# A two-layer decoder trunk on one core: low parts of the first 24 dense expert tiles of each layer made on GpSimd instead of VectorE

## The chip, the core and the metric

The kernel runs on one core of a Trainium2 chip. Time is device microseconds (us) of one execution, and less is better. TensorE (PE) multiplies, VectorE (DVE), ScalarE (ACT) and GpSimd (POOL) do the element-wise work, and SyncE (SP) starts most of the transfers from HBM. Three executions of the kernel before took 3294.35, 3295.38 and 3302.20 us; the median is 3295.38 us.

## What is computed

Two post-norm layers over 512 tokens of 1024 numbers. The first layer mixes tokens by retention, the second by differential attention, and each is followed by the same expert layer, PEER, in which the change lies:

```python
def peer_ffn(x, w_q, subkeys, u, v):      # per 128 tokens
    q = (xc @ w_q).reshape(128, 8, 2, 128)
    sc = einsum('thpd,hpnd->thpn', q, subkeys)
    s1, i1 = top_k(sc[:, :, 0], 16)
    s2, i2 = top_k(sc[:, :, 1], 16)
    cand = s1[..., :, None] + s2[..., None, :]
    cidx = i1[..., :, None] * 128 + i2[..., None, :]
    top, pos = top_k(cand.reshape(128, 8, 256), 16)
    idx = take_along_axis(cidx, pos)      # 8 x 16 experts of 16384
    gate = softmax(top)
    act = gelu(einsum('ted,td->te', u[idx], xc))
    return einsum('te,ted->td', gate * act, v[idx])
```

Every token picks 16 experts for each of 8 heads out of 16384. An expert is a row of `u` and a row of `v`, 1024 float32 numbers each.

## The kernel before

**Split numbers.** Matrix products are made at float32 accuracy from rounded halves. `split` (lines 102 to 104) has ACT round a tile to `h` (line 103), and then DVE, or another engine given as `eng`, subtracts to get the low part `l` (line 104). `mm3` (lines 106 to 109) adds three products, high by high, high by low and low by high. `wload` (line 111) loads a weight tile of 128x1024 into one of RING = 9 buffers `wraw` and splits it into `wh` and `wl`, of which there are three each. Weights of the query projections already get their low part on POOL, since `query_feed` hands `nc.gpsimd` to `wload`.

**The expert layer.** `peer` (line 879) treats the tokens as four blocks of 128. Block 0 is sparse: each of its 128 expert slots is one gather of rows of `u` by POOL (`ug`, line 752) and one dot product on DVE (line 754), later the same with `v` (lines 765, 767). Blocks 1 to 3, 384 tokens, are dense: PE multiplies all 128 tiles of 128 experts with the tokens (`u_tile`, line 854, 24 products of 128x384 per tile), ACT applies gelu, and the activations are weighted with a gate matrix that DVE, ACT and PE build from one-hot rows (`gmat`, line 827).

**The stage around the change.** The first part of `peer` (pool `p1`) does three things beside each other. DVE finds the best keys of each half (`topk_keys`, lines 685 to 690), sorts the pairs of them block by block (`topk_pairs`, lines 693 to 739) and then makes the one-hot rows of `gmat`. PE works through `u` tiles 0, 1, 2 and so on; 82 of the 128 are made here in each layer. From tile 22 on, dot products of block 0 are mixed in. The loop from line 941 gives the sequence: for each planned piece of DVE work `u_tile` calls are made until a planned tile time catches up, and the call `next(su)` issues a gather and a dot product behind the newest low part (`behind("low")`).

**Who sets the order on an engine.** The code is handed to a scheduler that orders each engine's instructions by its own model of their times. That order is fixed in the built program: an engine works its list in sequence, and an instruction that waits holds up all behind it. The program has the kernel's line numbers; `tk_` tiles belong to the pair sort, `sc` and `tk_m` to the key sort, `mu` and `rt` are the two PSUM tags that `u` tiles alternate on.

Of the kernel before, what the change touches and what calls it, by code (L numbers as in the profile page):

```python
# [54 lines left out]
OHB = 4  # L55
EQB = 2
UT = 4.0
RING = 9
SB = 4
LEAD = 4  # L60
# [3 lines left out]
def build(tc, I, out):  # L64
    nc = tc.nc
    ctx = ExitStack()
    with ctx:
# [21 lines left out]
        def bank(tag):  # L89
            return psum.tile([P, 512], F32, name=tag, tag=tag, bufs=4 if tag == "pj" else 2)  # L90
# [4 lines left out]
        def behind(*what):  # L95

            ctx = ExitStack()
            for w in what:
                ctx.enter_context(tc.issue_after(newest[w].ins))
            return ctx  # L100

        def split(h, l, src, eng=None):
            nc.scalar.activation(h, src, AF.Copy)  # L103
            newest["low"] = (eng or nc.vector).tensor_tensor(out=l, in0=src, in1=h.bitcast(F32), op=OP.subtract)  # L104

        def mm3(o, ah, al, bh, bl, start, stop):
            nc.tensor.matmul(o, ah, bh, start=start, stop=False)  # L107
            nc.tensor.matmul(o, ah, bl, start=False, stop=False)  # L108
            return nc.tensor.matmul(o, al, bh, start=False, stop=stop)  # L109

        def wload(src, eng=None, pool=None, tag="", bufs=3, dst=None):
            a = src.shape[1]
            pool = pool or wp
            raw = wp.tile([P, 1024], F32, name="wraw", tag="wraw", bufs=RING)
            nc.sync.dma_start(raw.rearrange("p (a b) -> p a b", a=a), src)
            if dst is None:
                h = pool.tile([P, 1024], F32R, name="wh", tag="wh" + tag, bufs=bufs)
                l = pool.tile([P, 1024], F32R, name="wl", tag="wl" + tag, bufs=bufs)
            else:
                h, l = dst  # L120
            split(h, l, raw, eng)
            return h.rearrange("p (a b) -> p a b", a=a), l.rearrange("p (a b) -> p a b", a=a)
# [67 lines left out]
        def lnp(l, i):  # L190
            g = wp.tile([P, D], F32, name="lng", tag="wraw", bufs=RING)
            nc.sync.dma_start(g, I["ln_g"][l, i:i + 1, :].to_broadcast([P, D]))
            b = wp.tile([P, D], F32, name="lnb", tag="wraw", bufs=RING)
            nc.sync.dma_start(b, I["ln_b"][l, i:i + 1, :].to_broadcast([P, D]))
            return g, b
# [46 lines left out]
        def retention():  # L242
            with tc.tile_pool(name="ret", bufs=1) as rp:
# [11 lines left out]
                def load_x(q):  # L255
                    xr = wp.tile([P, 1024], F32, name="wraw", tag="wraw", bufs=RING)
                    xr = xr.rearrange("p (a b) -> p a b", a=2)
                    nc.sync.dma_start(xr, I["xt"][:, 2 * q:2 * q + 2, :])
                    split(XTH[:, 2 * q:2 * q + 2, :], XTL[:, 2 * q:2 * q + 2, :], xr)
# [481 lines left out]
        def softmax(gate):  # L741
            nc.scalar.activation(gate, gate, AF.Exp)
            zs = small.tile([P, 8], F32, name="tk_z", tag="tk_z")
            nc.vector.reduce_sum(out=zs, in_=gate, axis=AX.X)
            nc.vector.reciprocal(out=zs, in_=zs)
            nc.vector.tensor_tensor(out=gate, in0=gate, in1=zs.unsqueeze(2).to_broadcast([P, 8, 16]), op=OP.mult)

        def sparse_u(kp, t, l, idx, act):
            scr = kp.tile([P, D], BF16, name="scr", tag="scr")
            for j in range(P):  # L750
                u = wp.tile([P, D], F32, name="ug", tag="wraw", bufs=RING)
                nc.gpsimd.indirect_dma_start(out=u, out_offset=None, in_=I[f"u{l}"],  # L752
# [5 lines left out]
        def sparse_v(kp, t, l, idx, gate, act):  # L758
# [4 lines left out]
            for j in range(P):  # L763
                v = wp.tile([P, D], F32, name="vg", tag="wraw", bufs=RING)
                nc.gpsimd.indirect_dma_start(out=v, out_offset=None, in_=I[f"v{l}"],  # L765
# [85 lines left out]
                nc.sync.dma_start(gd.rearrange("g p q f -> q p g f")[t0 // GT + q], st.rearrange("p (g a) t -> p g (a t)", a=GA))  # L851
                yield 6.0

        def u_tile(dp, l, a, tag="mu"):
            uh, ul = wload(I[f"ut{l}"][a])
            b = bank(tag)
            for k in range(KD):
                newest["mm"] = mm3(b[:, :DT], uh[:, k, :], ul[:, k, :], XTH[:, k, S - DT:], XTL[:, k, S - DT:], k == 0, k == KD - 1)
            act = dp.tile([P, DT], F32, name="uact", tag="uact", bufs=LEAD + 1)
            newest["gelu"] = nc.scalar.activation(act, b[:, :DT], AF.Gelu_apprx_tanh)  # L860
            return act
# [17 lines left out]
        def peer(l, norm, feed, prepare):  # L879
            with tc.tile_pool(name="sp", bufs=1) as sp, tc.tile_pool(name="dp", bufs=1) as dp:  # L880
# [6 lines left out]
                with tc.tile_pool(name="p1", bufs=1) as kp:  # L887
                    M = [kp.tile([P, 16, 16], F32, name=f"tk_m{t}") for t in range(TB)]
                    MI = [kp.tile([P, 16, 16], U32, name=f"tk_i{t}") for t in range(TB)]
                    with tc.tile_pool(name="pq", bufs=1) as qp:  # L890
                        scores(qp, M, MI, l, norm, feed)
                        if l == 0:
                            iota_f = qp.tile([P, P], F32, name="iota_f")
                            nc.sync.dma_start(iota_f, I["iota"])
                            nc.vector.tensor_copy(out=iota50,
                                                  in_=iota_f[:, :NCAND].unsqueeze(2).to_broadcast([P, NCAND, 16]))
                            nc.vector.tensor_copy(out=iota4, in_=iota_f.unsqueeze(2).to_broadcast([P, P, 4]))
                    with tc.tile_pool(name="tk", bufs=1) as tp:
                        def pairs(t, got):
                            idx = tp.tile([P, P], I32, name="tk_idx", tag="tk_idx", bufs=2)  # L900
                            gate = tp.tile([P, 8, 16], F32, name="tk_g", tag="tk_g", bufs=2)
                            yield from topk_pairs(tp, M[t], MI[t], idx, gate)
                            got.append((idx, gate))

                        def gates():


                            got = []

                            def exps():  # L910
                                with behind("gelu"):
                                    softmax(got[-1][1])

                            def rows():
                                with behind("mm"):
                                    return gate_rows(tp, got[-1][0], got[-1][1].rearrange("p h k -> p (h k)"))

                            yield from pairs(1, got)
                            yield 36.0
                            exps()  # L920
                            yield 8.0
                            nxt = rows()
                            yield 4.0
                            for t in range(1, TB):
                                now = nxt
                                more = pairs(t + 1, got) if t + 1 < TB else ()
                                for n, cost in enumerate(gmat(tp, *now, (t - 1) * P, gd, G0)):
                                    yield cost
                                    for c in (more if n == P // GT - 4 else itertools.islice(more, 2)):
                                        yield c  # L930
                                    if t + 1 < TB and n == P // GT - 3:
                                        exps()
                                    if t + 1 < TB and n == P // GT - 2:
                                        nxt = rows()

                        for _ in topk_pairs(tp, M[0], MI[0], idx0, gate0):
                            pass
                        su = sparse_u(sp, 0, l, idx0, act0)
                        nu, nd, tv, tu = 0, 0, 0.0, -40.0

                        for cost in gates():
                            tv += cost
                            while tu < tv and nu < P:
                                act = u_tile(dp, l, nu, ("mu", "rt")[nu % 2])
                                nc.sync.dma_start(ad[nu], act)
                                nu += 1
                                tu += UT
                                while nd < DOTS * (nu - LAG):
                                    with behind("low"):
                                        next(su, None)  # L950
                                    nd += 1
                                    tv += 1.2
                with tc.tile_pool(name="p2", bufs=1) as kp:
# [25 lines left out]
                    for a in range(P):  # L979
# [6 lines left out]
                        if a < nu:  # L986
                            act = kp.tile([P, DT], F32, name="aact", tag="aact", bufs=4)
                            nc.sync.dma_start(act, ad[a])
                        else:
                            act = ahead.pop(0)  # L990
# [97 lines left out]
```

## Time and profile before

| | |
|---|---|
| median of three executions | 3295.38 us |
| the profiled execution's own time | 3296.86 us |
| its span, first to last instruction | 3295.1 us |
| PE busy | 3200.2 us (97%) |
| DVE busy | 2519.7 us (76%) |
| ACT busy | 1397.7 us (42%) |
| POOL busy | 940.8 us (29%) |

The profile is one execution. The busy share of an engine is an average over stages that have different limits, so a stage is read by its own window. A row of a timeline gives the start, the duration, the engine, the line, the operation and, in square brackets, the idle time before it and what ended that.

### The profile page before, as it was taken

The numbers are of one execution on the slowest core, as the hardware profiler recorded it, in microseconds if no ns is written. First come the engines' busy times: TensorE is split into PE (matmuls) and PEld (weight loads), VectorE is DVE, ScalarE is ACT, GpSimd is POOL, SyncE is SP. The second block draws the span as 40 slices with busy tenths as digits, with TensorE's granted clock in tenths as the row PEclk, the third lists the DMA queues.
The fourth block names the chain that finished last, engine by engine and source line by source line (L and its number), as shares of the span: only waits on it lengthen the run. The fifth ranks groups of instructions, "written<-read, shape, count | busy, mean of one in ns | idle before, by whom it ended". The sixth has DMA issues, their size and how long they took to land.

```text
span 3295.1 us, 47178 instructions
## 1 busy us (share of the span) xinstructions
PE 3200.2 (97%) x16666; PEld 2844.1 (86%) x16666; DVE 2519.7 (76%) x4849; ACT 1397.7 (42%) x2436; POOL 940.8 (29%) x663
## 2 busy tenths in 40 slices
PE   9999999899989999999999999999999999999998
PEld 7888889899988888889888668989999788888987
DVE  4444468999768888888963665899986888888886
ACT  3323333367773333333333643335776333333332
POOL 1101330211112333455424423021111233345540
PEclk9999999999999999999999999999999999999999
DMA  5222233578789999999943202357878999999993
GB/s 212 86 86 85 90 94 127 183 235 259 250 267 342 360 354 349 330 359 357 352 140 92 77 26 84 120 175 235 250 257 264 336 355 365 342 334 344 354 341 134
DMA packets 310077, 774.38 MB, mean 235 GB/s; under 512 B 25936, under 2 KB 154320, under 8 KB 306256
## 3 DMA queue, kind: packets, MB, share of 16 engines
q1 hardware_dynamic: 236112, 502.89, 44.3%
q0 software_dynamic: 73728, 268.47, 22.6%
q8 instruction: 131, 2.15, 0.3%
q14 instruction: 106, 0.87, 0.1%
HBM read 692.88 MB, written 78.38 MB: 234 GB/s over the span
## 4 chain that ended last, share of the span: by engine, by line
PE 76%; DVE 12%; issue 8%; ACT 2%; DMA 1%; POOL 1%; POOLq 0%; DVEq 0%; SPq 0%; ACTq 0%
PE pj L107 13%; PE pj L108 13%; PE pj L109 13%; PE mu L109 6%; PE mu L107 6%; PE mu L108 5%; PE rt L108 5%; PE rt L107 5%; PE rt L109 5%; DVE wl L104 3%; PE pj L844 2%; DVE tk_idf L736 1%; DMA ug<-in_u,idx 1%; DVE tk_ex L733 1%; PE mu L499 1%
## 5 line engine op out<-in xcount | busy, mean ns | idle before, releaser
L103 ACT ACTIVATE wh<-wraw 128x1024 fp32r<-128x1024 f32 x632 | 659.3, 1055 | 609.9 <-PE mu L108 123.1
L104 DVE TENSOR_TENSOR wl<-wraw,wh 128x1024 fp32r<-128x1024 f32 x572 | 695.0, 1224 | 214.0 <-ACT wh L103 212.3
L752 POOL DMA_INDIRECT ug<-in_u,idx x256 | 355.5, 1389 | 1241.2 <-DVE wl L104 641.5
L107 PE MATMUL mu<-xth,wh 128*128 128x384 f32 (+1 forms) x1424 | 483.3, 340 | 25.7 <-ACT uact L860 18.4
L109 PE MATMUL mu<-xth,wl 128*128 128x384 f32 (+1 forms) x1424 | 482.3, 339 | 15.4 <-DVE wl L104 15.4
L108 PE MATMUL mu<-xtl,wh 128*128 128x384 f32 (+1 forms) x1424 | 480.3, 337 | 0.0
L765 POOL DMA_INDIRECT vg<-in_v,idx x256 | 336.1, 1313 | 329.6 <-DVE x L767 232.9
L108 PE MATMUL pj<-wl,wwh 128*128 128x512 f32 x1024 | 398.7, 390 | 0.0
L109 PE MATMUL pj<-wh,wwl 128*128 128x512 f32 x1024 | 397.2, 389 | 0.0
L103 ACT ACTIVATE wwh<-w 128x384 fp32r<-128x384 f32 x256 | 134.2, 525 | 602.2 <-issue 366.0
L107 PE MATMUL pj<-wh,wwh 128*128 128x512 f32 x1024 | 380.2, 390 | 0.0
L754 DVE CUSTOM_DVE_ANT_0 scr<-ug,x 128x1024 bf16<-128x1024 f32 x256 | 312.5, 1221 | 26.2 <-DMA ug<-in_u,idx 25.8
L767 DVE SCALAR_TENSOR_TENSOR x<-vg,wgt,x 128x1024 f32<-128x1024 f32 x256 | 328.3, 1282 | 4.2 <-DMA vg<-in_v,idx 0.7
L107 PEld LDWEIGHTS mu<-xth,wh 128*128 128x128 f32 x1424 | 271.2, 191 | 32.2 <-ACT uact L860 19.0
L109 PEld LDWEIGHTS mu<-xth,wl 128*128 128x128 f32 x1424 | 271.2, 190 | 20.4 <-DVE wl L104 20.2
L108 PEld LDWEIGHTS mu<-xtl,wh 128*128 128x128 f32 x1424 | 271.3, 191 | 3.6
L104 DVE TENSOR_TENSOR wwl<-w,wwh 128x384 fp32r<-128x384 f32 x256 | 142.7, 559 | 127.5 <-ACT wwh L103 123.0
L109 PE MATMUL rt<-xth,wl 128*128 128x384 f32 (+1 forms) x688 | 230.7, 335 | 7.2 <-DVE wl L104 7.2
L107 PE MATMUL rt<-xth,wh 128*128 128x384 f32 (+1 forms) x688 | 231.9, 338 | 0.2
L108 PE MATMUL rt<-xtl,wh 128*128 128x384 f32 (+1 forms) x688 | 230.2, 335 | 0.4 <-DVE xtl L104 0.4
L109 PEld LDWEIGHTS pj<-wh,wwl 128*128 128x128 f32 x1024 | 192.2, 188 | 40.1
L108 PEld LDWEIGHTS pj<-wl,wwh 128*128 128x128 f32 x1024 | 192.2, 188 | 38.5
(242 smaller groups left out, 6281.5 us busy)
## 6 DMA issues: line engine op xcount, KB each, us to landing
wraw<-in_ut SPq DMA_DIRECT2D x256, 512.0 KB, 4.5
wraw<-in_v SPq DMA_DIRECT2D x256, 512.0 KB, 6.9
gd<-g_st SPq DMA_DIRECT2D x48, 896.0 KB, 5.6
gl<-gd SPq DMA_DIRECT2D x28, 1536.0 KB, 9.7
ad<-uact SPq DMA_DIRECT2D x164, 192.0 KB, 3.2
aact<-ad SPq DMA_DIRECT2D x164, 192.0 KB, 5.4
wraw<-in_w_in SPq DMA_DIRECT2D x48, 512.0 KB, 4.2
wraw<-in_peer_w_q SPq DMA_DIRECT2D x32, 512.0 KB, 4.0
```

The lines of the kernel that those rows point to most:

```text
L103: nc.scalar.activation(h, src, AF.Copy)
L104: newest["low"] = (eng or nc.vector).tensor_tensor(out=l, in0=src, in1=h.bitcast(F32), op=OP.subtract)
L107: nc.tensor.matmul(o, ah, bh, start=start, stop=False)
L108: nc.tensor.matmul(o, ah, bl, start=False, stop=False)
L109: return nc.tensor.matmul(o, al, bh, start=False, stop=stop)
L499: nc.tensor.matmul(b[:, :n], qt[g][ms, h, qb * P:qb * P + P], kt[g][ms, h, :n], start=True, stop=True)
L733: nc.vector.tensor_tensor(out=ex, in0=eq, in1=cidx[:, hs, :].unsqueeze(3).to_broadcast([P, HG, NCAND, 16]), op=OP.mult)
L752: nc.gpsimd.indirect_dma_start(out=u, out_offset=None, in_=I[f"u{l}"], in_offset=bass.IndirectOffsetOnAxis(ap=idx[:, j:j + 1], axis=0))
L754: nc.vector.tensor_tensor_reduce(out=scr, in0=u, in1=X[t], scale=1.0, scalar=0.0, op0=OP.mult, op1=OP.add, accum_out=act[:, j:j + 1])
L765: nc.gpsimd.indirect_dma_start(out=v, out_offset=None, in_=I[f"v{l}"], in_offset=bass.IndirectOffsetOnAxis(ap=idx[:, j:j + 1], axis=0))
L767: nc.vector.scalar_tensor_tensor(out=X[t], in0=v, scalar=w[:, j:j + 1], in1=X[t], op0=OP.mult, op1=OP.add)
L844: nc.tensor.matmul(b[:, i * P:i * P + P], oh[:, 1, i, :], oh[:, 0, i, :], start=True, stop=True)
```

## The change

`u_tile` gets a parameter `eng`, which it hands to `wload`. In the loop of `peer` the first `EARLY` = 24 tiles of each layer pass `nc.gpsimd`, so that their low part is a subtraction on POOL; tiles 24 to 127 stay with DVE. Lines after 57 move down by two.

```diff
@@ -55,6 +55,8 @@
 UT = 4.0
+
+EARLY = 24
 RING = 9
@@ -851,8 +853,8 @@
-        def u_tile(dp, l, a, tag="mu"):
-            uh, ul = wload(I[f"ut{l}"][a])
+        def u_tile(dp, l, a, tag="mu", eng=None):
+            uh, ul = wload(I[f"ut{l}"][a], eng)
             b = bank(tag)
@@ -941,7 +943,7 @@
                             while tu < tv and nu < P:
-                                act = u_tile(dp, l, nu, ("mu", "rt")[nu % 2])
+                                act = u_tile(dp, l, nu, ("mu", "rt")[nu % 2], nc.gpsimd if nu < EARLY else None)
                                 nc.sync.dma_start(ad[nu], act)
```

The order on POOL, from the last weights of the retention to the end of the expert layer of layer 0; `ug` and `vg` are gathers, `rs_r` belongs to a layer norm. Before:

```order
L104 TENSOR_TENSOR wo<-wraw,wo 128x1024
L187 TENSOR_TENSOR rs_r<-rs_t,mhalf 128x1 x4
L104 TENSOR_TENSOR wl<-wraw,wh 128x1024 x13
L752 DMA ug<-in_u,idx_3192 128x1024 x128
L765 DMA vg<-in_v,idx_3192 128x1024 x128
```

And in the changed program:

```order
L106 TENSOR_TENSOR wo<-wraw,wo 128x1024
L189 TENSOR_TENSOR rs_r<-rs_t,mhalf 128x1 x4
L106 TENSOR_TENSOR wl<-wraw,wh 128x1024 x36
L754 DMA ug<-in_u,idx_3192 128x1024
L106 TENSOR_TENSOR wl<-wraw,wh 128x1024
L754 DMA ug<-in_u,idx_3192 128x1024 x127
L767 DMA vg<-in_v,idx_3192 128x1024 x128
```

The 13 low parts of query weights are followed by those of tiles 0 to 22, one gather, the low part of tile 23, and then the other gathers.

The order on DVE in the pair sort of block 0, from the products of positions and indices (`tk_ex`) on. Before, low parts stand between the sort's instructions:

```order
L733 TENSOR_TENSOR tk_ex<-tk_eq,tk_ci 128x1600 x2
L716 MAX tk_b<-tk_c 128x8 x8
L104 TENSOR_TENSOR wl<-wraw,wh 128x1024
L736 TENSOR_REDUCE tk_idf<-tk_ex 128x32
L104 TENSOR_TENSOR wl<-wraw,wh 128x1024
L736 TENSOR_REDUCE tk_idf<-tk_ex 128x32
L718 MAX_INDEX tk_p<-tk_b,tk_c 128x8 x8
L733 TENSOR_TENSOR tk_ex<-tk_eq,tk_ci 128x1600
```

In the changed program:

```order
L735 TENSOR_TENSOR tk_ex<-tk_eq,tk_ci 128x1600 x2
L718 MAX tk_b<-tk_c 128x8 x8
L738 TENSOR_REDUCE tk_idf<-tk_ex 128x32 x2
L720 MAX_INDEX tk_p<-tk_b,tk_c 128x8 x8
L735 TENSOR_TENSOR tk_ex<-tk_eq,tk_ci 128x1600 x2
L723 MATCH_REPLACE tk_c<-tk_b,tk_c 128x50 x8
```

The sort runs through without a low part from its beginning on.

The order on DVE around the first dot product of block 0 (`scr`, shown as ISA). Before, it stands in the middle of the second block's pair sort:

```order
L736 TENSOR_REDUCE tk_idf<-tk_ex 128x32
L104 TENSOR_TENSOR wl<-wraw,wh 128x1024
L754 ISA scr,act_3191<-ug,x_77 128x1024
L754 ISA act_3191 128x1
L736 TENSOR_REDUCE tk_idf<-tk_ex 128x32
L721 MATCH_REPLACE tk_c<-tk_b,tk_c 128x50 x8
L104 TENSOR_TENSOR wl<-wraw,wh 128x1024
```

In the changed program:

```order
L718 MAX tk_b<-tk_c 128x8 x8
L720 MAX_INDEX tk_p<-tk_b,tk_c 128x8 x8
L756 ISA scr,act_3191<-ug,x_77 128x1024
L756 ISA act_3191 128x1
L106 TENSOR_TENSOR wl<-wraw,wh 128x1024 x2
L756 ISA scr,act_3191<-ug,x_77 128x1024
L756 ISA act_3191 128x1
L106 TENSOR_TENSOR wl<-wraw,wh 128x1024
```

The two low parts behind the first dot product are those of tiles 24 and 25, the first that DVE still makes; ahead of them stand the whole pair sorts of blocks 0 and 1 and the first half (candidates and both passes for the best 16) of those of blocks 2 and 3.

## Rows read from the trace of the kernel before

**Rows 1.** The page: busy time by engine, and ACT's costliest group.

```profile
PE 3200.2 (97%) x16666; PEld 2844.1 (86%) x16666; DVE 2519.7 (76%) x4849; ACT 1397.7 (42%) x2436; POOL 940.8 (29%) x663
...
L103 ACT ACTIVATE wh<-wraw 128x1024 fp32r<-128x1024 f32 x632 | 659.3, 1055 | 609.9 <-PE mu L108 123.1
```

**Rows 2.** Waits of PE, whole run: total us, times, longest.

```profile
PE mu L109 <- DVE wl L104: 15.4, 13, 2.7
```

**Rows 3.** Busy time by window: window, its length, engines, granted clock, DMA share, GB/s.

```profile
544.00:621.00 77.00, 73.61 (x421) 72.47 (x420) 76.97 (x268) 25.60 (x36) 11.67 (x4) 1.00 0.50 163
659.00:741.00 82.00, 82.00 (x532) 82.00 (x531) 82.00 (x152) 54.52 (x112) 14.88 (x9) 1.00 0.73 235
```

**Rows 4.** Timeline of PE: first products of tiles 8, 9, 24 and 29.

```profile
557.14 0.33 PE L107 MATMUL mu<-xth,wh 128*128 128x384 f32 x1
...
561.30 0.33 PE L107 MATMUL rt<-xth,wh 128*128 128x384 f32 x1
...
632.08 0.33 PE L108 MATMUL rt<-xtl,wh 128*128 128x384 f32 x1
...
659.02 0.33 PE L108 MATMUL rt<-xtl,wh 128*128 128x384 f32 x1
```

**Rows 5.** Low parts that POOL already makes: duration ns, minimum, median, maximum.

```profile
L104 POOL TENSOR_TENSOR wl<-wraw,wh x60: 2354/2396/3007, 370.5 to 2076.3; 128x1024 fp32r<-128x1024 f32 x60
```

**Rows 6.** Groups of DVE instructions between 549.6 and 659.7 us.

```profile
L104 DVE TENSOR_TENSOR wl<-wraw,wh 128x1024 fp32r<-128x1024 f32 x23 | 28.3, 1234 | 0.8 <-ACT wh L103 0.8
L736 DVE TENSOR_REDUCE tk_idf<-tk_ex 128x32 f32<-128x1600 f32 x8 | 23.8, 2976 | 0.0
L733 DVE TENSOR_TENSOR tk_ex<-tk_eq,tk_ci 128x1600 f32<-128x1600 bf16 x8 | 14.5, 1833 | 0.0
...
L754 DVE CUSTOM_DVE_ANT_0 scr<-ug,x 128x1024 bf16<-128x1024 f32 x6 | 7.4, 1239 | 0.0
L730 DVE TENSOR_TENSOR tk_eq<-iota,tk_pb 128x1600 bf16<-128x1600 bf16 x8 | 7.4, 1003 | 0.0
```

**Rows 7.** Timeline of DVE: end of the key sort, start of the pair sort.

```profile
525.17 0.87 DVE L685 MAX8 tk_m<-sc 128x8 f32<-128x128 f32 x4 [2.68 <-ACT sc L808]
...
549.68 0.29 DVE L695 CAST tk_f<-tk_i 128x256 f32<-128x256 uint32 x1
```

**Rows 8.** Timelines of POOL and DVE where a low part on POOL meets DVE.

```profile
1802.24 2.43 POOL L104 TENSOR_TENSOR wl<-wraw,wh 128x1024 fp32r<-128x1024 f32 x1 [4.87 <-ACT wh L103]
...
1802.20 0.22 DVE L431 TENSOR_TENSOR tok<-rtmp 128x64 f32<-128x64 f32 x1
1802.33 2.42 DVE L432 TENSOR_TENSOR tok<-rtmp 128x64 f32<-128x64 f32 x1
...
451.73 2.39 POOL L104 TENSOR_TENSOR wl<-wraw,wh 128x1024 fp32r<-128x1024 f32 x1 [4.83 <-ACT wh L103]
...
452.08 0.28 DVE L687 FIND_INDEX8 tk_i<-tk_m,sc 128x8 uint32<-128x128 f32 x1
```

**Rows 9.** Timelines of POOL and DVE around three POOL instructions.

```profile
1651.36 1.55 POOL L187 TENSOR_TENSOR rs_r<-rs_t,mhalf 128x1 f32<-128x1 f32 x1 [17.23 <-DVE rs_t L185]
...
1651.25 3.50 DVE L104 TENSOR_TENSOR wl<-wraw,wh 128x1024 fp32r<-128x1024 f32 x3
...
601.85 7.20 POOL L752 DMA_INDIRECT ug<-in_u,idx  x1 [0.30 <-issue]
...
634.91 0.94 POOL L752 DMA_INDIRECT ug<-in_u,idx  x1 [4.37 <-DVE wl L104]
...
634.54 2.97 DVE L736 TENSOR_REDUCE tk_idf<-tk_ex 128x32 f32<-128x1600 f32 x1
```

**Rows 10.** A long wait of PE in its timeline, and two windows after it.

```profile
986.27 0.69 PE L107 MATMUL mu<-xth,wh 128*128 128x384 f32 x1 [9.46 <-ACT uact L860]
...
980.00:986.00 6.00, 0.00 (x0) 0.00 (x0) 5.34 (x6) 5.97 (x7) 3.24 (x2) 0.50 0.84 265
986.00:990.00 4.00, 3.73 (x12) 3.73 (x13) 4.00 (x7) 1.59 (x4) 2.63 (x3) 0.50 1.00 346
```

## The prediction, made before the changed kernel ran

> **What bounds the kernel now.** I read the page first: PE is busy for 97% of the span [rows 1], so a change on DVE or POOL counts only where PE waits for them. The list of PE's waits says where that is: for the tiles of one PSUM tag alone it waits 15.4 us, in 13 pieces, for low parts made by DVE [rows 2]. Then I read windows. During the pair sort DVE is busy for 76.97 of 77 us, while PE is not [rows 3]. From 659 us on PE is busy all the time as well, for 82.00 of 82 us [rows 3], and stays so nearly to the end of the layer. So a microsecond that PE gains or loses among the first 30 tiles of a layer is a microsecond of the end, once per layer, and the two layers look alike.
>
> How much is there? An undisturbed tile takes 561.30 - 557.14 = 4.16 us of PE [rows 4]. From tile 9 at 561.30 tile 24 could begin at 623.7 and tile 29 at 644.5. They begin at 632.08 and 659.02 [rows 4]. The stage loses 14.5 us per layer, waits and the slower clock after them together. Twice that, 29 us, is the most the change can win here.
>
> **The change, step by step.** It takes 24 subtractions per layer from DVE and gives them to POOL. Nothing is added: the same transfers, roundings and products. The scheduler, though, closes the gaps on DVE: in its new order the pair sort stands in one piece, and the low parts of tiles 24 and 25 come behind it.
>
> *POOL's own pace.* A low part takes 2.40 us on POOL [rows 5], 1.23 on DVE [rows 6]. With three buffers, tile n's can begin about 1.1 us into tile n-2, when ACT has rounded it, which takes 1.06 us [rows 1]. It then has 7.2 us until tile n begins and needs 2.4. The gathers queued behind tile 22's and 23's are not wanted before DVE is through its sort. I cost this at nothing; PE's patience is 4.8 us per tile, and what uses it up is a rival below.
>
> *DVE's start.* Eight low parts stand ahead of the pair sort, which begins at 549.68 [rows 7]. Three of them come before DVE runs dry and waits 2.68 us for scores [rows 7]; these win nothing. The other five, 1.14 us each from start to start, bring the sort forward by 5.7 us, to 544.0.
>
> *DVE's list up to the first dot product.* Before, the same work lay between 549.7 and 659.7 us: 110 us, with 23 low parts and 6 dot products in it [rows 6]. Without these 29 x 1.14 = 33 us it is 77 us. Undisturbed, DVE reaches the first dot product at 544 + 77 = 621 us, and tile 24's low part is ready at 623.3, just in time for 623.7.
>
> *What DVE loses to POOL.* This is where I expect the gain to go. Where a low part on POOL and an addition of two SBUF tensors on DVE meet, the DVE instruction, 0.22 us by itself, takes 2.42 us and ends with POOL's [rows 8]. A search in the key sort, which reads one tensor, takes its 0.28 us beside another low part [rows 8], and a reduction runs beside a POOL gather that still takes only 0.94 us [rows 9]. So I count as exposed what reads two SBUF tensors, with the casts: the products (8 at 1.74 us from start to start), the comparisons (8 at 0.90) and about 10 us of small additions and casts, 31 of the 77 us. The other 46 us, reductions, maxima and searches, run on.
>
> POOL makes the low parts of tiles 7 to 23 in this time: 17, one per 4.16 us, from 545.8 to 614.7. The first bound of what they cost DVE is nothing, if each falls beside a reduction or search; the second is 17 x 2.39 = 40.6 us, if each stops DVE from its first to its last moment. Between the two I take it in proportion. Of 4.16 us POOL holds 2.39, which leaves 1.77 for exposed work, so an exposed microsecond takes 2.35. In the 69 us DVE gets through y of free and 0.67 y of exposed work, with y + 0.67 y x 2.35 = 69: y = 26.7, together 44.7 us. It loses 24 us.
>
> *The sum.* DVE reaches the dot product at 544 + 77 + 24 = 645 us. With that and one low part, 1.14 us each, tile 24 begins at 647.6 instead of 632.1. PE has stood since 623.7. Five tiles later it is at 668.4 instead of 659.0: 9.4 us lost. After a long wait the clock is low for a while: after 9.46 us PE ran 3.8 us at a granted clock of 0.50, its 1.2 GHz level, up to 990.06 us, which cost 1.9 us [rows 10]. I add that, with the same row as the nearest: 11.3 us per layer, 22.6 in all. DVE's later work fits behind PE, since the list after the sort is no longer than before and PE comes later to it. On the profiled execution's 3296.9 us that makes 3319.5; the median of the runs is 1.5 us lower, so 3318. The bounds are 3266 (nothing lost) and 3350 (40.6 us lost).
>
> The break-even is worth knowing: tile 29 is on time if tile 24 begins at about 636, hence if DVE loses 13 us. **Below 13 us the change wins, above it loses.**
>
> **Rivals.**
>
> *The low parts hardly meet exposed work (faster).* If DVE loses under 5 us, PE never waits for POOL and at most 4 us at tile 24. With nothing lost tile 29 comes at 644.5, 14.5 us earlier, 29 us over two layers: 3266 against the median. With 5 us lost it is about 3276, with the clock 3280. For it: 46 of 77 us read one tensor, and reductions come in pairs of 5.8 us in the new order, long enough for a low part. Against it: the exposed work comes in blocks of up to 8 us, and POOL asks every 4.16 us.
>
> *DVE keeps POOL out through a whole run of exposed instructions (no change).* A gather that takes 0.94 us when free took 7.20, to the end of a run of additions and comparisons on DVE [rows 9]. If low parts on POOL wait like that, DVE loses only what sticks out behind a reduction or search, some 0.7 us of each, 12 in all. But then PE waits for POOL: a run of eight comparisons, products and additions lasts about 8.6 us, PE's patience is 4.8, so twice some 3 us are lost; DVE reaches the dot product at 633, and tile 29 comes near 656. Three waits, each with a spell of low clock that costs 1.7 us as those of the stage now do, make it 661, 2 us late: 3299 for two layers, between 3290 and 3305.
>
> Against that rival stands a small POOL instruction that met three low parts on DVE in a row: it ended 0.44 us after the first, while the others ran on, unlengthened [rows 9]. I take this as the more direct case, since it is an arithmetic instruction. The Trainium skill, page "SBUF — State Buffer", section "SBUF: two separate sides", says that DVE and GpSimd share a port pair that is an exclusive lock, held for one whole instruction by whoever starts first. By that rule a POOL instruction gets its turn after each DVE instruction, which is my forecast, 3318, and not 3299; the 2.42 us agree with the lock, and the 7.20 us do not agree with the turn.
>
> *Nearly every low part stops DVE in full.* 3335 to 3350; for this the proportion would have to be far off.
>
> **How the numbers follow.** About 0.3%, 10 us, is what a measurement of this kernel can tell from no change: 3285.5 to 3305.3. The forecast, 3308 to 3335 for 17 to 32 us lost, gets 0.55; DVE keeping POOL out, 3290 to 3305, gets 0.27; the gain, 3266 to 3287, gets 0.15; the full stop 0.03. Slower by over 0.3% is the forecast and the full stop, 0.58; no change is the second rival without its rim, 0.26; faster is 0.16. The range leaves out the gain and the full stop, nearly 0.2: 3286 to 3335. The forecast's own range is 3308 to 3335.
>
> **What the profile of the changed kernel would show.** PE's waits on DVE's low parts are no longer spread over the stage in pieces of 2 us: one wait of some 20 us per layer stands ahead of tile 24, with a granted clock of 0.50 behind it. DVE's products and comparisons have means well above 1.83 and 1.00 us, with single ones near 4, while reductions and searches keep theirs. The first dot product starts near 645 us. POOL's low parts stay under 4 us each. If instead their median in the sort is 5 us or more and PE waits for POOL at two places, the second rival is right. If the first dot product starts before 628 and PE runs through, the first is. I am wrong altogether if the time moves without tile 29 of layer 0 having moved, or if the second layer does something else than the first.

## The result: 0.5% slower, and the profile after

The changed kernel took 3314.77 us (median of six executions, 3307.88 to 3319.82), the kernel before, run beside it, 3298.95 us (six executions, 3294.35 to 3302.20). The ratio is 1.0051, 95% interval 1.0038 to 1.0064: slower, by 15.8 us. The prediction was 3318 us, with 0.58 on slower. The profiled execution of after is its longest, 3319.82 us.

Busy time by engine, from the page of after, answers to [rows 1]:

```profile
PE 3199.7 (96%) x16666; PEld 2848.6 (86%) x16666; DVE 2510.4 (76%) x4801; ACT 1395.9 (42%) x2436; POOL 1067.1 (32%) x711
```

PE's work is the same. DVE gave up 48 low parts of 1.23 us, 59 us, and yet its busy time fell by only 9 us: 50 us were put on it elsewhere. The waits of PE for low parts of the tag `mu`, whole run (total us, times, longest), against the 15.4 us in 13 pieces of [rows 2]:

```profile
PE mu L111 <- DVE wl L106: 50.8, 9, 23.7
```

Before, PE's waits for low parts between 500 and 800 us, the stage of layer 0, were these, 8.5 us with both tags:

```profile
PE mu L109 <- DVE wl L104: 4.9, 3, 2.7
PE rt L109 <- DVE wl L104: 3.6, 2, 2.1
```

Now the stage of each layer has a single wait, two of the nine; this is layer 0's in PE's timeline (start, duration, and in brackets the idle time and what ended it), with the first products of tile 24 ahead of it and tile 29 behind, and then layer 1's:

```profile
626.01 0.33 PE L109 MATMUL mu<-xth,wh 128*128 128x384 f32 x1
626.19 0.34 PE L110 MATMUL mu<-xtl,wh 128*128 128x384 f32 x1
650.18 0.69 PE L111 MATMUL mu<-xth,wl 128*128 128x384 f32 x1 [23.66 <-DVE wl L106]
...
675.12 0.33 PE L109 MATMUL rt<-xth,wh 128*128 128x384 f32 x1
...
2234.36 0.69 PE L111 MATMUL mu<-xth,wl 128*128 128x384 f32 x1 [21.33 <-DVE wl L106]
```

PE starts tile 24 at 626.01, does the two products that need only the high part, and stands until DVE has made the low part. The windows say the same (columns as in [rows 3]): no PE loss in the sort, where before 3.4 of 77 us were lost [rows 3], a clock of 0.50 right behind the wait, and a PE that is busy all the time from tile 29 to 757 us.

```profile
546.00:621.00 75.00, 75.00 (x435) 75.00 (x434) 74.91 (x218) 25.88 (x36) 57.14 (x19) 1.00 0.40 137
...
650.00:655.00 5.00, 4.82 (x15) 4.82 (x16) 4.99 (x9) 0.00 (x0) 2.61 (x2) 0.50 0.76 249
675.00:757.00 82.00, 82.00 (x537) 82.00 (x536) 81.11 (x109) 56.11 (x123) 14.78 (x9) 1.00 0.77 255
```

A tile is counted here by PE's products, 24 for each. That is how [rows 4] has to be read as well: the rows at 632.08 and 659.02 are the products with 24 and 29 tiles' worth of work ahead of them, and not the first products of tiles 24 and 29, since before the products of neighbouring tiles are mixed (the row at 632.08 has the tag `rt` and line 108, which belong to an odd tile and to a second product). As marks of PE's progress the rows of before and after can be compared.

One thing must be taken off before the two traces are compared. In this execution the clock was down for a moment at 392 us, ahead of the stage (window, engines, granted clock as above):

```profile
392.00:395.60 3.60, 3.60 (x10) 2.78 (x9) 1.31 (x3) 1.02 (x2) 2.36 (x1) 0.54 0.52 157
```

The first product of tile 0 starts 2.9 us late, 1.7 of it by the clock (3.60 us at 0.54). Up to 497 us all kernels here have the same instructions in the same order on PE, DVE, ACT and POOL, so this is not the change's work; nine of the eleven traces of after and of the experiments have this dip, and the one trace of before does not. PE's timeline of before, at the first product of tile 0 in layers 0 and 1, and at the first one after the stage of layer 1:

```profile
519.64 0.33 PE L107 MATMUL mu<-xth,wh 128*128 128x384 f32 x1
2093.24 0.33 PE L107 MATMUL mu<-xth,wh 128*128 128x384 f32 x1
2559.39 0.69 PE L107 MATMUL mu<-xth,wh 128*128 128x384 f32 x1 [8.94 <-ACT uact L860]
```

The row of layer 0's end stands in [rows 10], 986.27. PE's timeline of after, at the start and the end of the stage in both layers:

```profile
522.57 0.33 PE L109 MATMUL mu<-xth,wh 128*128 128x384 f32 x1
998.12 0.69 PE L109 MATMUL mu<-xth,wh 128*128 128x384 f32 x1 [9.37 <-ACT uact L862]
2109.08 0.33 PE L109 MATMUL mu<-xth,wh 128*128 128x384 f32 x1
2582.72 0.69 PE L109 MATMUL mu<-xth,wh 128*128 128x384 f32 x1 [9.97 <-ACT uact L862]
```

Layer 0 begins 2.9 us late and ends 11.9 late: the stage lost 8.9 us. Layer 1 begins 15.8 late and ends 23.3 late: 7.5 us. Together 16.4 us, against 15.8 between the medians. The rest of the 23 us between the two spans lies outside the stage, 2.9 us ahead of it and 4.0 between the two. Between the layers the clock fell at two places where before it did not (columns as in [rows 3]); the two windows of after, and below them one of before that takes in all of that stretch:

```profile
1447.00:1450.40 3.40, 2.96 (x9) 2.97 (x10) 3.37 (x4) 0.30 (x1) 2.13 (x2) 0.50 0.60 189
1518.70:1522.10 3.40, 3.40 (x12) 3.39 (x12) 3.33 (x4) 0.00 (x0) 1.81 (x2) 0.51 0.65 187
...
991.00:1867.00 876.00, 867.72 (x4119) 739.95 (x4117) 668.91 (x980) 318.66 (x493) 337.69 (x244) 1.00 0.79 289
```

The 4.0 us are not this execution's alone: in all eleven traces the stretch between the layers is 3.1 to 7.9 us longer than in the one trace of before, with spells at 0.50 between 1425 and 1590 us. Why the clock falls there, and whether other executions of before have it too, is not shown. So the stage explains the change's loss, but that 16.4 lies so near to 15.8 is in part chance: this execution is 5 us above the median of its kernel.

Where most of DVE's 50 us went (20 and 18 us in the sorts of the two layers, over the run with one eighth below) shows in its groups between the start of the sort and the first dot product (us busy, mean ns), layer 0:

```profile
L738 DVE TENSOR_REDUCE tk_idf<-tk_ex 128x32 f32<-128x1600 f32 x8 | 23.2, 2937 | 0.0
L735 DVE TENSOR_TENSOR tk_ex<-tk_eq,tk_ci 128x1600 f32<-128x1600 bf16 x8 | 14.4, 1841 | 0.0
...
L707 DVE TENSOR_TENSOR tk_c<-tk_m 128x16 f32<-128x16 f32 x12 | 10.5, 922 | 0.0
L732 DVE TENSOR_TENSOR tk_eq<-iota,tk_pb 128x1600 bf16<-128x1600 bf16 x8 | 7.4, 984 | 0.0
L697 DVE CAST tk_f<-tk_i 128x256 f32<-128x256 uint32 x4 | 5.3, 1322 | 0.1
```

Reductions, products and comparisons have the means of [rows 6]. It is the small additions of line 707 and the casts of line 697 that grew: a mean of 922 ns for 16 numbers per partition, and 1322 ns for a cast that took 0.29 us before [rows 7]. One such place in the timelines of POOL and of DVE:

```profile
560.66 11.07 POOL L106 TENSOR_TENSOR wl<-wraw,wh 128x1024 fp32r<-128x1024 f32 x3 [1.75 <-ACT wh L105]
```

```profile
560.50 0.64 DVE L707 TENSOR_TENSOR tk_c<-tk_m 128x128 f32<-128x128 f32 x4
561.05 3.70 DVE L732 TENSOR_TENSOR tk_eq<-iota,tk_pb 128x1600 bf16<-128x1600 bf16 x4
564.66 7.20 DVE L707 TENSOR_TENSOR tk_c<-tk_m 128x24 f32<-128x24 f32 x4
571.78 0.21 DVE L711 TENSOR_TENSOR tk_c<-tk_m 128x64 f32<-128x64 f32 x1
```

POOL's low part starts at 560.66 and is kept out by the rest of four additions and by four comparisons, which run at their usual pace; it takes 6.36 us, the longest in the run (POOL's low parts, minimum, median, maximum in ns):

```profile
L106 POOL TENSOR_TENSOR wl<-wraw,wh x108: 2350/2400/6362, 371.9 to 2205.2; 128x1024 fp32r<-128x1024 f32 x108
```

Then POOL gets its turn, makes three low parts end on end until 571.73, and four additions of 0.2 us take 7.20 us together: POOL's next low part was ready each time, and each of the first three additions lasted until one of them ended.

### The profile page after: what moved, and what is told of

It reads as the page before. It is cut to its first block, busy times and chain, and to the rows that moved or that the text cites. A ratio compares the mean times of both kernels' runs of the same rounds, so it can differ in the third digit from the quotient of the medians.

```text
span 3318.1 us, 47188 instructions
## 1 busy us (share of the span) xinstructions
PE 3199.7 (96%) x16666; PEld 2848.6 (86%) x16666; DVE 2510.4 (76%) x4801; ACT 1395.9 (42%) x2436; POOL 1067.1 (32%) x711
## 4 chain that ended last, share of the span: by engine, by line
PE 81%; DVE 9%; issue 6%; ACT 1%; DMA 1%; POOL 1%; POOLq 0%; SPq 0%; DVEq 0%; ACTq 0%
PE pj L109 13%; PE pj L110 13%; PE pj L111 13%; PE mu L111 6%; PE mu L109 6%; PE mu L110 6%; PE rt L110 6%; PE rt L109 6%; PE rt L111 6%; PE pj L846 3%; DVE tk_idf L738 1%; DMA ug<-in_u,idx 1%; DVE tk_c L707 1%; PE mu L501 1%; PE rt L808 1%
## 5 line engine op out<-in xcount | busy, mean ns | idle before, releaser
L106 DVE TENSOR_TENSOR wl<-wraw,wh 128x1024 fp32r<-128x1024 f32 x524 | 636.7, 1224 | 225.7 <-ACT wh L105 219.1
L754 POOL DMA_INDIRECT ug<-in_u,idx x256 | 341.5, 1334 | 1052.1 <-DVE wl L106 611.7
L106 POOL TENSOR_TENSOR wl<-wraw,wh 128x1024 fp32r<-128x1024 f32 x108 | 283.3, 2628 | 332.5 <-ACT wh L105 307.9
```

## The experiments

All kernels are edits of the changed one; the one with one eighth and the copy leave work out. In the seven rows under the change DVE's order up to the first dot product is that of the change. "Sort" is the time from the first cast of the pair sort to the first dot product, layer 0 of the one profiled execution.

| run | sort, us | median, us | ratio to before, 95% interval |
|---|---|---|---|
| the change (24 tiles) | 100.8 | 3314.8 | 1.0051 (1.0038 to 1.0064) |
| one eighth on GpSimd | 80.5 | 3275.8 | 0.9927 (0.9912 to 0.9942) |
| copy on GpSimd | 83.0 | 3282.4 | 0.9951 (0.9935 to 0.9966) |
| four pieces, 24 tiles | 91.8 | 3297.7 | 0.9997 (0.9987 to 1.0006) |
| 28 tiles | 102.5 | 3295.4 | 0.9994 (0.9984 to 1.0003) |
| two pieces, 28 tiles | 96.2 | 3285.0 | 0.9967 (0.9954 to 0.9979) |
| four pieces, 28 tiles | 96.7 | 3288.3 | 0.9974 (0.9964 to 0.9984) |
| eight pieces, 28 tiles | 109.7 | 3312.3 | 1.0049 (1.0033 to 1.0066) |
| 8 tiles (15 low parts of DVE in the sort) | 80.5 | 3291.8 | 0.9976 (0.9966 to 0.9986) |
| 14 tiles (9 low parts in it) | 90.1 | 3304.3 | 1.0017 (1.0008 to 1.0026) |
| 16 tiles (7 low parts in it) | 90.5 | 3309.7 | 1.0033 (1.0023 to 1.0043) |

The theory: GpSimd's low parts stop DVE's additions, and what DVE loses in the sort PE waits for. Its first rival: the new order costs the time by itself.

**One eighth of the work on GpSimd.**

```diff
-            split(h, l, raw, eng)
+            nc.scalar.activation(h, raw, AF.Copy)
+            p = slice(0, piece)
+            newest["low"] = (eng or nc.vector).tensor_tensor(out=l[:, p], in0=raw[:, p], in1=h[:, p].bitcast(F32), op=OP.subtract)
...
-            uh, ul = wload(I[f"ut{l}"][a], eng)
+            uh, ul = wload(I[f"ut{l}"][a], eng, piece=128 if eng else 1024)
...
-                newest["mm"] = mm3(b[:, :DT], uh[:, k, :], ul[:, k, :], XTH[:, k, S - DT:], XTL[:, k, S - DT:], k == 0, k == KD - 1)
+                newest["mm"] = mm3(b[:, :DT], uh[:, k, :], (uh if eng and k else ul)[:, k, :], XTH[:, k, S - DT:], XTL[:, k, S - DT:], k == 0, k == KD - 1)
```

> The part on GpSimd of each of the 24 low parts is cut to one eighth (128x128 in place of 128x1024); the products of the other seven eighths take the high part instead of the low one, so PE, ACT and the transfers do the same work and the low part of the weights is left out. DVE's order up to the first dot product is that of the change. Theory port (GpSimd's low parts stop DVE's additions of two SBUF tensors until they end): from the start of the pair sort to the first dot product it takes 78 to 84 us in place of 101.7, no addition takes over 0.6 us, PE waits under 5 us for tile 24's low part, and the time is 3266 to 3280 us, faster than the kernel before by 15 to 30 us. Rival order (the sort in one piece, with tile 24's low part behind it, costs the time by itself): the sort still takes over 95 us, PE still waits 20 us or more, 3305 to 3320 us. Rival handover (each instruction on GpSimd costs DVE a fixed time, however short): 95 us or more too, with additions still near 2.4 us.

The sort took 80.5 us, PE's wait shrank to 3.4 us, and the time came to 3275.8 us. DVE's groups in the sort, and PE's wait between 500 and 800 us:

```profile
L737 DVE TENSOR_TENSOR tk_ex<-tk_eq,tk_ci 128x1600 f32<-128x1600 bf16 x8 | 14.2, 1819 | 0.0
...
L709 DVE TENSOR_TENSOR tk_c<-tk_m 128x16 f32<-128x16 f32 x12 | 2.0, 218 | 0.0
...
L699 DVE CAST tk_f<-tk_i 128x256 f32<-128x256 uint32 x4 | 1.2, 300 | 0.1
```

```profile
PE mu L111 <- DVE wl L125: 3.4, 1, 3.4
```

With the same order, and the same count of GpSimd instructions, the additions are back at 218 ns and the cast at 300. So neither the order nor a fixed price per instruction costs the time; it is the time that GpSimd's instruction lasts. Without what that takes from DVE, the move of the low parts and the new order, both together, would be worth 22 us.

**Four pieces per low part.**

```diff
-            split(h, l, raw, eng)
+            nc.scalar.activation(h, raw, AF.Copy)
+            for i in range(0, 1024, piece):
+                p = slice(i, i + piece)
+                newest["low"] = (eng or nc.vector).tensor_tensor(out=l[:, p], in0=raw[:, p], in1=h[:, p].bitcast(F32), op=OP.subtract)
...
-            uh, ul = wload(I[f"ut{l}"][a], eng)
+            uh, ul = wload(I[f"ut{l}"][a], eng, piece=256 if eng else 1024)
```

> GpSimd makes each of the 24 low parts in four pieces of 128x256, the same work in shorter instructions; DVE's order is that of the change. Theory port: no addition on DVE takes over 0.8 us, since GpSimd holds the port for about 0.6 us at a time; GpSimd has to win the port four times for one low part, so DVE loses less than in the change, 8 to 20 us of sort instead of 22 to 25, and the time is 3280 to 3312 us. Rival order: no change against the changed kernel, 3310 to 3320 us. Rival handover (a fixed price per GpSimd instruction): more is lost than in the change, 3325 us or more.

91.8 us of sort, 3297.7 us, no addition over 0.85 us: as the theory had it, but for the 0.8. The four kernels with 24 tiles and one order on DVE (the copy is told below) now stand near a line: 80.5, 83.0, 91.8 and 99.6 us of sort (the last the mean of 100.8 and layer 1's 98.4) give 3275.8, 3282.4, 3297.7 and 3314.8 us. That is 39.0 us for 19.1, 2.04 us for each microsecond that DVE loses in a layer (2.6, 1.7 and 2.2 in the single steps); there are two layers. The traces say it of the stage alone: from the run with one eighth to the change it grows by 21.6 us in layer 0, for 20.3 of sort, and by 18.9 in layer 1, for 18.0. And the break-even is where a sort of 91.8 us gives the time of before.

**The copy.**

```diff
+            if copy:
+                nc.scalar.activation(h, raw, AF.Copy)
+                newest["low"] = eng.tensor_copy(out=l, in_=raw)
+            else:
+                split(h, l, raw, eng)
...
-            uh, ul = wload(I[f"ut{l}"][a], eng)
+            uh, ul = wload(I[f"ut{l}"][a], eng, copy=bool(eng))
```

> GpSimd copies the tile (one tensor read, one written) where the change subtracts; the subtraction is left out, and so the output is not that of the low parts. DVE's order up to the first dot product is that of the change. Theory whole port (whatever GpSimd does in SBUF holds DVE's additions until it ends): additions of up to the copy's own length, and a loss in the sort that is to the 22 us of the change as the copy's length is to 2.40 us, at least 5 us. Rival two operands (only GpSimd instructions that read two tensors stop DVE): no addition over 0.6 us, the first dot product 78 to 82 us after the sort's start, 3266 to 3282 us as in the run with one eighth.

Neither expectation holds in full. Three copies in the sort, from POOL's timeline:

```profile
559.25 2.55 POOL L125 CAST wl<-wraw 128x1024 fp32r<-128x1024 f32 x1 [3.11 <-PE rt L111]
563.41 3.10 POOL L125 CAST wl<-wraw 128x1024 fp32r<-128x1024 f32 x1 [1.61 <-PE mu L111]
567.58 1.05 POOL L125 CAST wl<-wraw 128x1024 fp32r<-128x1024 f32 x1 [1.06 <-PE rt L111]
```

Beside a reduction a copy takes 1.05 us; beside comparisons and products it waits, 2.55 and 3.10. Four additions of DVE lasted over 1 us, none over 1.07. So here a POOL instruction that reads one tensor meets DVE's additions too, and stops one for about its own length. But DVE lost only 2.5 us over the run with one eighth, less than the 5 that the first theory wanted, and 3282.4 us lies just above the rival's range. How much of that is the shorter instruction and how much the single operand stays open.

**Fewer tiles.** `EARLY = 24` becomes 8, 14 or 16.

> EARLY = 8: only the low parts that are made beside the key sort, which reads one tensor, move to GpSimd. Theory port: DVE's additions stay under 0.4 us, the pair sort starts some 5.7 us earlier than in the kernel before, tile 29 of each layer starts 5 us earlier, and the time is 3283 to 3291 us. Rival order: low parts still stand between DVE's sort instructions, so no single wait of 20 us; also 3283 to 3291. A time of 3295 or more would say that the start of the sort isn't what sets tile 29, against both.

The time was 3291.8 us, just outside. One low part of GpSimd still met the sort (one addition of 2.42 us), and PE still waited 8.2 us in the stage, in pieces of up to 2.5. The gain, 5.7 us, is half of what the earlier start alone promised. In the trace the stage itself did gain that, 5.0 and 5.9 us in the two layers; 5.5 us were lost ahead of the stage and between the layers, as in the other traces.

> EARLY = 16: about nine low parts per layer on GpSimd meet the pair sort, seven stay beside the key sort. Theory port: DVE saves 5.7 us at the start of the sort and 9.1 us in it, and loses about 9/17 of the 22 to 25 us that it loses in the change, 12 us: 3 us per layer to the good, 3286 to 3300 us, with several additions near 2.4 us. Rival order: DVE's order again has low parts between the sort's instructions, so nothing is lost and the gain is 12 to 14 us per layer: 3267 to 3275 us.

3309.7 us, slower than before by 12 us. Both expectations missed. The waits of PE in layer 0, and POOL's timeline at the place:

```profile
PE rt L111 <- POOL wl L106: 11.0, 1, 11.0
PE mu L111 <- DVE wl L106: 5.7, 2, 3.3
PE rt L111 <- DVE wl L106: 1.7, 1, 1.7
```

```profile
595.96 1.12 POOL L754 DMA_INDIRECT ug<-in_u,idx  x1 [16.43 <-DVE tk_p L720]
597.12 2.35 POOL L106 TENSOR_TENSOR wl<-wraw,wh 128x1024 fp32r<-128x1024 f32 x1
```

The low part of tile 15 stands on POOL behind the first gather, and the gather waits 16.43 us for the indices that DVE's sort makes. I took this queue for the cause and set EARLY to 14, where no low part stands behind a gather.

> EARLY = 14. In the run with 16, PE waited 11 us per layer for tile 15's low part, which stood on GpSimd behind the first gather, and the gather waited for DVE's indices; with 14 all low parts of GpSimd stand ahead of the gathers. Theory queue (that wait is what made 16 slower than before): no wait of PE for GpSimd, DVE loses 7 to 11 us in the sort to 7 low parts and saves 5 to 6 at its start and 6.8 for six low parts fewer, so 0 to 4 us per layer to the good: 3287 to 3298 us. Rival port alone (what DVE loses makes 16 slower): 3303 to 3312 us here too.

3304.3 us, in the range of the rival that I had set up against it: the queue was not needed for the loss, though it may have a part in the 5 us by which 16 tiles are slower than 14. The waits of PE in layer 0:

```profile
PE mu L111 <- DVE wl L106: 12.2, 1, 12.2
PE rt L111 <- DVE wl L106: 2.6, 1, 2.6
```

Now PE waits 12.2 us for tile 14, the first low part that DVE makes itself. By then DVE had lost some 11 us in the sort: four additions took 2.41 to 2.43 us and a cast 2.36, which take 0.3 or less by themselves. In the runs with 14, 16 and 24 tiles PE waits, at the first place where it needs DVE in the sort, for about all that DVE has lost by then.

**More tiles.** `EARLY = 24` becomes 28.

> EARLY = 28: the low parts of tiles 24 to 27 move to GpSimd as well, ahead of the gather that waits for a free buffer; the first low part of DVE is that of tile 28, behind three dot products. Theory port: DVE reaches the first dot product some 2 to 5 us later than in the change (GpSimd's low parts meet the sort to its end), near 650 to 653, and the low part of tile 28 near 660; PE waits for it once, from 640 to 660, as long as in the change but four tiles later, so the time is 3295 to 3310 us, better than the change by 5 to 18 us and not better than the kernel before by over 3 us. Rival order (it is the place of tile 24's low part behind the sort): with that place moved four tiles on, 16 us per layer are won, PE waits under 8 us, 3280 to 3288 us.

3295.4 us, at the edge of the theory's range, and the wait is another than the one I expected:

```profile
PE rt L822 <- DVE tk_g L748: 9.8, 1, 9.8
PE rt L822 <- DVE g_if L819: 3.7, 1, 3.7
```

PE no longer waits for a low part, but for the gates that it transposes for the gate matrix (line 822), which are DVE's too and stand around the first dot products. The loss moved to the next thing that is DVE's, 13.5 us in place of 23.7. The same trace has a place where POOL holds DVE, in DVE's and in POOL's timeline:

```profile
622.26 7.30 DVE L735 TENSOR_TENSOR tk_ex<-tk_eq,tk_ci 128x1600 f32<-128x1600 bf16 x2
```

```profile
621.38 4.76 POOL L106 TENSOR_TENSOR wl<-wraw,wh 128x1024 fp32r<-128x1024 f32 x2
```

Two products, 3.7 us by [rows 6], take 7.30. The first stood from 622.26 until POOL was through with two low parts, at 626.14, not with one.

**Pieces and 28 tiles.** The edit for four pieces with EARLY at 28 and `piece` at 256, 512 or 128.

> EARLY = 28 and four pieces of 128x256 per low part on GpSimd. Theory port: the first dot product comes 92 to 98 us after the sort's start as in the run with pieces and 24 tiles, near 638 to 641; the low part of tile 28 stands behind three dot products, near 646 to 650, and PE, due at 640.4, waits 5 to 10 us. Tile 29 starts at 650 to 655 in place of 659: 4 to 9 us per layer to the good, 3279 to 3290 us, faster than the kernel before. If GpSimd is kept out so long that PE waits for its pieces, or the gathers come late, 3293 or more.

3288.3 us, as expected and faster than both kernels; but the one wait of PE in the stage, 7.9 us, is again for the gates and not for tile 28.

> EARLY = 28, two pieces of 128x512 per low part on GpSimd. With four pieces DVE took 96.7 us from the sort's start to the first dot product, with one 102.5. Theory turns (the port goes over at the end of each instruction): the loss follows the length of a piece; 98 to 101 us, additions of up to 1.3 us, 3288 to 3295 us. Rival gap (it goes over only where an engine has no next instruction ready): two pieces run back to back and hold it as long as one whole low part, so 101 to 104 us, 3293 to 3298 us.

> EARLY = 28, eight pieces of 128x128 per low part on GpSimd. Theory turns: 90 to 95 us from the sort's start to the first dot product in place of 96.7, no addition over 0.6 us, 3278 to 3287 us. Rival gap: a run of eight pieces holds the port as long as four do, and GpSimd's own time grows with the number of pieces, so 96 to 101 us, single products of DVE near 4 us, 3287 to 3296 us.

With two pieces 96.2 us and 3285.0 us, the lowest of all that leave nothing out, though its interval and that of four pieces overlap; additions of up to 3.05 us (3.22 in layer 1). With eight pieces 109.7 us and 3312.3 us. Both theories called two pieces worse than four, and neither was right there. For eight pieces the turns were wrong by far, and the gap was right in kind and too small. DVE's and POOL's timeline with eight pieces:

```profile
577.88 19.07 DVE L738 TENSOR_TENSOR tk_ex<-tk_eq,tk_ci 128x1600 f32<-128x1600 bf16 x2
```

```profile
572.67 20.59 POOL L126 TENSOR_TENSOR wl<-wraw,wh 128x128 fp32r<-128x128 f32 x49
```

POOL works 49 pieces without a gap, until 593.26. A product of DVE that could start at 577.88 ends at 594.94, after 17.06 us, 1.7 us behind the last piece. Eight pieces take 8 x 20.59 / 49 = 3.4 us in place of 2.40, so POOL, once late, always had the next piece to do, and DVE did not get in between two of them. Why two pieces did no worse than four stays open.

## Why the prediction was right

Taken with the 2.9 us off that the execution was late, step by step:

- *DVE's start:* forecast 544.0, measured 546.98 - 2.9 = 544.1. The 5.7 us are there; with four pieces and 24 tiles, where tile 0 starts as before (519.65), it was 544.07 as it stands.
- *DVE's list to the first dot product:* forecast 77 us of work and 24 us lost, 101 together; measured 100.8, and 98.4 in layer 1. The division is less sure. With one eighth on GpSimd the list takes 80.5 us, so the loss is between 20 us (over that run) and 24 (over my 77).
- *The dot product:* forecast 645, measured 647.77 - 2.9 = 644.9. Tile 24's products go on at 650.18 - 2.9 = 647.3, forecast 647.6.
- *Tile 29 and the clock:* forecast 668.4 and 1.9 us of low clock, 670.3; measured 675.12 - 2.9 = 672.2. PE had stood 23.66 us in the midst of tile 24, and the clock was at 0.50 up to 655.1, for 4.9 us of work. That is 2.5 us, where I took 1.9 from the shorter wait of [rows 10].
- *The sum:* forecast 11.3 us per layer, measured 8.9 and 7.5. This is the term that was off, by 2.4 and 3.8 us. By tile 29 layer 0 had lost 672.2 - 659.0 = 13.2 us. But in the new order 16 products of the gate matrix (1.7 us at 0.108 each) stood ahead of tile 29 that used to come behind it, and a wait of 1.8 us that PE had for a one-hot row at 758.6 is gone. That leaves 9.7, of which 0.8 more came back where I can't name it. I had said that later work fits behind PE and had not looked for what it would give back. Layer 1's wait is 2.3 us shorter than layer 0's. The forecast was 22.6 us slower, and 15.8 were measured; that the time itself came within 3.2 us of 3318 is luck in part, since the kernel before, run beside the changed one, took 3298.95 us and not the 3295.38 that the sum starts from.
- *POOL's own pace, costed at nothing:* right, PE never waited for a low part of POOL. But the sign that I gave, low parts under 4 us, was wrong: three of layer 0's took 4.58, 5.02 and 6.36 us, and PE's patience covered them.

One of the signs failed, and with it a reason. I expected products and comparisons near 4 us; they kept their means of 1.84 and 0.98. The second rival was right about that: a run of such instructions keeps POOL out, as the gather of [rows 9] had shown. I had set against it the small POOL instruction of [rows 9], which got its turn after one low part. The Trainium skill, page "SBUF — State Buffer", section "SBUF: two separate sides", calls the shared port an exclusive lock that is held for a whole instruction. That the other side's turn comes next I had read into it; the section does not say so. The additions of 2.42 us agree with the lock. The product that waited behind some 36 pieces (15.2 us at 0.42) does not agree with a turn. The rival's price for DVE, 12 us, was wrong all the same, because POOL works off its arrears when the run of comparisons ends and the small additions begin: each addition then waits for a whole low part. Taking the loss in proportion to time gave the right sum for a division of it that I had wrong: of the 31 us counted as exposed only the additions and casts, about 10 us, were stretched, single ones to ten times their length. That the sum came out right all the same is luck.

The break-even, 13 us lost on a list of 77, is 90 us of sort. The run with four pieces and 24 tiles had 91.8 and ended at 0.9997 of the kernel before; in its trace the two stages together are 2.1 us shorter than before, and the stretch between the layers is 3.6 us longer.

## What to carry to other kernels

Before work is moved from DVE to GpSimd, count what it does to DVE where the two meet: here a low part made beside the sort took some 1.1 to 1.2 us from DVE (20.3 us over 17 low parts in layer 0, 18.0 in layer 1), and DVE makes one itself in 1.14. The scheduler here closed the gaps in DVE's list, and then every microsecond that DVE was late was about one of PE, at whatever PE next needed from it. Moving that place (28 tiles) or cutting the length of one stop (four pieces) each brought the time back to that of the kernel before, and only both together went below it (0.9967 and 0.9974); taking one particular wait out (14 tiles in place of 16) left the kernel slower than before (1.0017). Moving nothing but the first 8 low parts, nearly all made beside the key sort, is as good (0.9976) and far simpler: a search of that sort took 0.28 us beside a low part of POOL and without one. Smaller pieces are not better without end: with eight they ran without a gap, stopped DVE for as long as the run lasted, and took longer.

## What the runs showed of the hardware that was not expected

- POOL and DVE do not always take turns instruction by instruction. DVE kept a low part of POOL out through the end of four additions and four comparisons (6.36 us in place of 2.40), and POOL kept a product of DVE out for 15 us through a run of 128x128 pieces (17.06 us in all). Yet additions of 0.2 us and low parts alternated, one to one, at 564.66 to 571.73 us. What decides between the two was not settled.
- Short POOL instructions cost more per number: 0.42 us for 128x128 in the run without gaps, 2.40 for eight times as much.
- The long DVE instructions that read two tensors were stretched only when POOL was already at work as they came up (the product of 5.57 us with 28 tiles, that of 17.06 us with eight pieces); the short ones, 0.16 to 0.3 us, took nearly all of the loss in the changed kernel: 15 us on additions and 4 on casts, against the run with one eighth.
